# The start of a hybrid SSD and delta-rule step: x loaded in pieces from two queues, the first norm in halves, and the scaled x made on one engine

## The chip, the cores and the metric

The kernel runs on one core of one Trainium2 chip. The metric is device microseconds of one execution. The engines are PE (TensorE, matrix products and transposes), DVE (VectorE), ACT (ScalarE), POOL (GpSimd) and SP (SyncE, which here issues nearly all DMAs). DMAs can also be issued from ACT.

## What is computed

One inference step of a single-layer encoder. A prompt of 16 learned meta tokens and 256 tokens, and a sample of 64 tokens, 336 rows of 2048 in all, run through one layer:

```python
u = _rmsnorm(x, norm_mix_w)                     # x * rsqrt(mean(x*x) + EPS) * w, row by row
z_a, xbc_a, dt_a, qkv_b, z_b, beta_b, a_b, gate_a, gate_b = jnp.split(u @ w_in, SPLIT_IDX, axis=-1)
# branch A: causal conv, SiLU, SSD scan over blocks of 64, gated norm     -> ya
# branch B: causal conv, SiLU, gated delta rule over blocks of 64, norm   -> ob
mix = sigmoid(gate_a) * (ya @ w_out[:2048]) + sigmoid(gate_b) * (ob @ w_out[2048:])
h = x + mix
h = h + square(relu(_rmsnorm(h, norm_mlp_w) @ w_up)) @ w_down
```

Then a last RMSNorm. The outputs are y of the prompt and of the sample and the new conv and scan states of both. All data are float32.

## The kernel before

All 336 rows stand side by side on the free axis, and features on the partitions, 128 at a time. A float32 product is made of three: every operand is split into a rounded part (hi) and its rest (lo), and PE adds hi*hi, hi*lo and lo*hi. Weights come in a fixed stream of pieces of 512 KB (`stream`): `wload` (L193) loads piece n into one of three `raw` buffers, `wsplit` (L201) makes hi on ACT and lo on DVE (on POOL for n = 3) in three buffers each. `block` (L213) multiplies four pieces with all rows: at piece n it loads piece n + 3, whose buffer comes free when piece n is split, and splits the pieces up to n + 2. A piece feeds 24 matmuls.

This case is about the start, up to the first block of the first projection. Three tiles x0, x1, x2 of 112 rows each are loaded (`load_x`, L291; `segs` names the row ranges of the sources). For each tile the sum of squares is taken (`sumsq`, L321: x0 on ACT, x1 on DVE, x2 in halves on both), the root is made (`root`, L334: mean on DVE, power on POOL), 16 transposes on PE bring the tile to features on partitions (`flip`, L328, four at a time into one PSUM buffer) and ACT or DVE copies them to xT. A diagonal matrix of the roots (`spread_d`) is multiplied with ones on PE, so that the roots of all 336 rows stand on every partition: prx, copied to rbx. Then, for each of the 16 features groups k, `u_scale` (L380) makes ut = xT * rbx, and `u_split` (L384) makes uh on ACT and ul on DVE:

```python
def u_scale(k):
    ut[k] = sp0.tile([P, NT], F32, tag="ut", name="ut", bufs=6)
    tt(G if k % 2 else V, ut[k], xT[k // 4][:, k % 4, :], rbx, MUL)
```

The loop at L464 runs `u_split(k)` and `u_scale(k + 4)`, splits weight pieces 1 to 3 on the way, and issues two steps of three matmuls of block 0 for each k. Behind block 0, PE's order is written out: the transposes of small parameter rows to columns (pcol, from the loads cra, crb, sra, srb), the 32 matmuls of the token projection (ptok, with the weights wt split into wtr), and then the next blocks, pbig again.

From L344 to L472 the order on every engine is as written (`manual_schedule`). Instructions outside may be put among them: for all engines but PE a planner orders them ahead of the run by when it expects them to be ready, and by their place in the program among those that are ready. An engine then runs its instructions in that order, SP too. Before this stretch stand the loads of x and of prow; behind it, in the program's order: cra, crb, sra, srb, the two halves of dvec, four loads of pb, two of wt (L475 to L504). dvec, pb and wt are used by the scan, by `nega` (an Exp of pb on ACT, L528) and by the token projection. dvec is made of single floats, one half for each parity of the head:

```python
for h in range(2):
    nc.sync.dma_start(dvec[h * 64:(h + 1) * 64, :], i["ssd_d"][0].rearrange("(t h) -> h t", h=2)[h].partition_broadcast(64))
```

`scratch` (L996) stores the 16 tiles of xT to DRAM and clears twelve DRAM regions from the tile zero.

Of the kernel before, what the change touches and what calls it, by code (L numbers as in the profile page):

```python
# [8 lines left out]
F32 = mybir.dt.float32  # L9
F32R = mybir.dt.float32r  # L10
AF = mybir.ActivationFunctionType
ALU = mybir.AluOpType
# [3 lines left out]
D = 2048  # L16
KD = D // P
# [7 lines left out]
EPS = 1e-6  # L25
# [17 lines left out]
def tile_hybrid_step(ctx: ExitStack, tc: tile.TileContext, i: dict, o: dict):  # L43
    nc = tc.nc
# [9 lines left out]
    def scr(name):  # L54
        return pss.tile([P, 512], F32, tag="sc", name=name)

    def mm(out, lhsT, rhs, start=True, stop=True, **kw):
        nc.tensor.matmul(out, lhsT=lhsT, rhs=rhs, start=start, stop=stop, **kw)  # L58

    def act(out, in_, func=AF.Copy, **kw):  # L60
        nc.scalar.activation(out=out, in_=in_, func=func, **kw)  # L61

    def tt(eng, out, a, b, op):
        eng.tensor_tensor(out=out, in0=a, in1=b, op=op)  # L64
# [4 lines left out]
    V, G = nc.vector, nc.gpsimd  # L69
    MUL, ADD, SUB = ALU.mult, ALU.add, ALU.subtract  # L70
# [5 lines left out]
    ident = const.tile([P, P], F32, name="ident")  # L76
    make_identity(nc, ident)
    ones = const.tile([P, P], F32, name="ones")
# [6 lines left out]
    def transp(out, in_):  # L85
        n = in_.shape[0]
        nc.tensor.transpose(out, in_, ident[:n, :n])
# [10 lines left out]
    def new_u(name):  # L98
        return (keep.tile([P, KD, NT], F32R, tag="uh", name=name + "h"),
                keep.tile([P, KD, NT], F32R, tag="ul", name=name + "l"))  # L100

    uh, ul = new_u("u")
    acc = keep.tile([P, KD, NO], F32, name="acc")

    par = const.tile([P, 73], F32, name="par")
# [4 lines left out]
    dvec = const.tile([P, 16], F32, name="dvec")  # L110
# [82 lines left out]
    def wload(n):  # L193
        if n >= len(stream) or n in raws:
            return
        raw = wpool.tile([P, 4, 256], F32, tag="raw", name="raw", bufs=3)
        for c0, src in stream[n]:
            nc.sync.dma_start(raw[:, :, c0:c0 + src.shape[1]], src.rearrange("(k p) c -> p k c", p=P))
        raws[n] = raw

    def wsplit(n):  # L201
        if n >= len(stream) or n in split:
            return
        wload(n)
        hi = wpool.tile([P, 4, 256], F32R, tag="hi", name="hi", bufs=3)
        act(hi, raws[n])
        lo = wpool.tile([P, 4, 256], F32R, tag="lo", name="lo", bufs=3)
        tt(G if n == 3 else V, lo, raws[n], hi.bitcast(F32), SUB)
        split[n] = hi, lo
# [62 lines left out]
    sp0 = start.enter_context(tc.tile_pool(name="sp0", bufs=1))  # L272
# [3 lines left out]
    zero = sp0.tile([P, 4 * DG // P], F32, name="zero")  # L276
# [11 lines left out]
    xs = []  # L288
    segs = [[(0, "meta", 0, 16), (16, "pr", 0, 96)], [(0, "pr", 96, 112)], [(0, "pr", 208, 48), (48, "sa", 0, 64)]]
    src = {"meta": i["meta_tokens"], "pr": i["x_prompt"][0], "sa": i["x_sample"][0]}  # L290
    def load_x(n):  # L291
        for p0, s, r0, nr in segs[n]:
            nc.sync.dma_start(xs[n][p0:p0 + nr, :], src[s][r0:r0 + nr, :])

    for n in range(3):
        xs.append(xp.tile([112, D], F32, name=f"x{n}"))
    load_x(0)
    load_x(1)
    prow = sp0.tile([73, P], F32, name="prow")
    for r0, name, nr in ((NM, "norm_mix_w", 16), (SN, "ssd_norm_w", 16), (NP_, "norm_mlp_w", 16), (CB_, "ssd_conv_b", 24), (GN, "gdn_norm_w", 1)):  # L300
        nc.sync.dma_start(prow[r0:r0 + nr, :], i[name][0].rearrange("(t c) -> t c", c=P))
    load_x(2)
    warm = sp0.tile([P, 1], F32, name="warm")
    act(warm, ones[:, 0:1], AF.Square)

    def load_cols(dst, row, n):
        ps = scr("pcol")
        transp(ps[:, :n], row[:n, :])
        V.tensor_copy(dst, ps[:, :n])


    xT = [cpool.tile([P, 4, NT], F32, tag=t, name="xT", bufs=b) for t, b in (("q", 2), ("k", 2), ("v", 1))]
    xT.append(sp0.tile([P, 4, NT], F32, name="xT3"))
    junk = acc.rearrange("p k n -> p (k n)")[:112, :]
    ssx = sp0.tile([112, 4], F32, name="ssx")
    rsx = sp0.tile([112, 3], F32, name="rsx")
    dgx = sp0.tile([112, 3, 112], F32, name="dgx")
    rbx = sp0.tile([P, NT], F32, name="rbx")
    HD = D // 2

    def sumsq(f, x, d0, n):  # L321
        d = junk[:, d0:d0 + x.shape[1]]
        if f is act:
            act(d, x, AF.Square, accum_out=ssx[:, n:n + 1])
        else:
            V.scalar_tensor_tensor(out=d, in0=x, scalar=1.0, in1=x, op0=MUL, op1=MUL, accum_out=ssx[:, n:n + 1])

    def flip(n, k):  # L328
        ps = scr("pu").rearrange("p (k t) -> p k t", k=4)[:, :, :112]
        for m in range(4):  # L330
            transp(ps[:, m, :], xs[n][:, (k + m) * P:(k + m + 1) * P])
        return xT[k // 4][:, :, n * 112:(n + 1) * 112], ps

    def root(n):  # L334
        r = rsx[:, n:n + 1]
        V.tensor_scalar(out=r, in0=ssx[:, n:n + 1], scalar1=1.0 / D, scalar2=EPS, op0=MUL, op1=ADD)
        tt(G, r, r, nhalf_pow[:112, 0:1], ALU.pow)

    def spread_d(n):
        V.tensor_scalar(out=dgx[:, n, :], in0=ident[:112, :112], scalar1=rsx[:, n:n + 1], scalar2=None, op0=MUL)  # L340

    manual = ExitStack()
    manual.enter_context(tc.manual_schedule())

    pw_ = scr("pwarm")
    for n in range(8):
        mm(pw_[:, :P], ident, ident)
    prx = psb.tile([P, 512], F32, tag="big", name="prx")
    sumsq(act, xs[0], 0, 0)
    for k in range(0, KD, 4):  # L350
        (V.tensor_copy if k < 8 else act)(*flip(0, k))
    root(0)
    sumsq(V, xs[1], D, 1)
    for k in range(0, KD, 4):
        act(*flip(1, k))
    root(1)
    load_cols(par, prow, 73)
    for n in range(3):
        wload(n)
    sumsq(act, xs[2][:, :HD], 0, 2)  # L360
    sumsq(V, xs[2][:, HD:], D, 3)
    tt(V, ssx[:, 2:3], ssx[:, 2:3], ssx[:, 3:4], ADD)
    root(2)
    spread_d(0)
    spread_d(1)
    act(*flip(2, 0))
    late = [flip(2, k) for k in (4, 8, 12)]
    spread_d(2)
    wsplit(0)
    for n in range(3):  # L370
        mm(prx[:, n * 112:(n + 1) * 112], ones[:112, :], dgx[:, n, :])
    act(rbx, prx[:, :NT])
    for a in late:
        act(*a)
    xctx.close()
    sp = start.enter_context(tc.tile_pool(name="sp", bufs=1))
# [1 line left out]
    ut = {}  # L378

    def u_scale(k):  # L380
        ut[k] = sp0.tile([P, NT], F32, tag="ut", name="ut", bufs=6)
        tt(G if k % 2 else V, ut[k], xT[k // 4][:, k % 4, :], rbx, MUL)

    def u_split(k):  # L384
        t, w = ut.pop(k), par[:, NM + k:NM + k + 1]
# [76 lines left out]
    for k in range(4):  # L462
        u_scale(k)
    for k in range(KD):  # L464
        u_split(k)
        if k + 4 < KD:
            u_scale(k + 4)
        if k % 4 == 1 and k < KD - 4:
            wsplit(k // 4 + 1)
        for _ in range(2 if k < KD - 1 else 1):  # L470
            next(main0)
# [12 lines left out]
    srb_src = i["state_gdn_conv"][0, 0].rearrange("k (t c) -> (k t) c", c=P)  # L484
    for n in range(2):
        nc.sync.dma_start(srb[n], srb_src[n * 72:(n + 1) * 72, :])
    for h in range(2):
        nc.sync.dma_start(dvec[h * 64:(h + 1) * 64, :], i["ssd_d"][0].rearrange("(t h) -> h t", h=2)[h].partition_broadcast(64))
    pb = sp.tile([P, 2, 48], F32, name="pb")
# [16 lines left out]
    for n in range(2):  # L506
        w, wr = wt[:, n * 8:(n + 1) * 8, :], wpool.tile([P, 8, P], F32R, tag="hi", name="wtr", bufs=3)
# [697 lines left out]
    with tc.manual_schedule():  # L1205
        for t in range(3):
            final_part(7, t)
            r, n = frs[:, t:t + 1], toks[t][1]
            stt(r[n], fss[n, t, 7:8], 1.0 / D, fsum[n, t:t + 1], MUL, ADD)
            tt(G, r[n], r[n], nhalf_pow[n, 0:1], ALU.pow)  # L1210
        for m in range(2):
            for t, (_, n, t0) in enumerate(toks):
                dst = o["y_prompt"][0, t0:t0 + P, :] if t < 2 else o["y_sample"][0]
                w, r = slice(m * H, (m + 1) * H), frs[n, t:t + 1]
# [36 lines left out]
```

## Time and profile before

| | us |
|---|---|
| median of 3 runs (2331.62 to 2332.45) | 2331.97 |
| the profiled execution | 2331.78 |
| its span in the profile | 2330.1 |
| DVE busy | 1360.9 (58%) |
| ACT busy | 1064.6 (46%) |
| POOL busy | 333.0 (14%) |

The profile is of one execution. Times are counted from the start of the span; a busy PE is one that has matmuls in its pipeline, at whatever clock. PEclk is the granted clock of TensorE: 1.00 is 2.4 GHz, 0.50 is 1.2 GHz. A bracket behind a row tells how long the engine had been idle and what ended that.

### The profile page before, as it was taken

The page shows a single profiled execution, that of the slowest core. Times are in us where ns is not written, and L with a number is a line of the kernel's source. Part 1 is how long each engine was busy: PE and PEld are TensorE (multiplying, and loading weights), DVE is VectorE, ACT ScalarE, POOL GpSimd, SP SyncE. Part 2 cuts the span into 40 slices and gives each one's busy share as a digit, 9 for nine tenths or more (in the row PEclk, how much of TensorE's full clock was granted, in tenths as well). Part 3 has the DMA queues.
Part 4 walks back from the last instruction along what each step waited for, and adds up shares of the span by engine and source line. Part 5 has one row for each costly group of instructions (what it writes and reads, how often), then busy time and mean ns, then how long its engine had stood idle before and what let it go on. Part 6 is the DMA issues. An engine that isn't in the chain of part 4 may idle for free.

```text
span 2330.1 us, 40632 instructions
## 1 busy us (share of the span) xinstructions
PE 2300.5 (99%) x16393; PEld 2278.1 (98%) x16393; DVE 1360.9 (58%) x2147; ACT 1064.6 (46%) x1830; POOL 333.0 (14%) x488
## 2 busy tenths in 40 slices
PE   7999999999999999999999999999999999999997
PEld 7999999999999999999999999999999999999997
DVE  6674858585865547658668467444444444444444
ACT  5655546455445545554554445433343244324433
POOL 3151505041211102212212110000000000000000
PEclk8999999999999999999999999999999999999999
DMA  7846555545575555555546644544554444445543
GB/s 194 225 121 188 143 159 150 159 135 173 156 200 170 148 164 139 154 150 144 156 148 165 170 142 145 154 149 151 148 154 149 150 148 151 154 146 153 168 141 117
DMA packets 411046, 362.87 MB, mean 156 GB/s; under 512 B 48329, under 2 KB 407834, under 8 KB 410394
## 3 DMA queue, kind: packets, MB, share of 16 engines
q1 hardware_dynamic: 410746, 360.15, 53.1%
q8 instruction: 128, 2.10, 0.4%
q14 instruction: 60, 0.49, 0.1%
q10 hardware_dynamic: 112, 0.13, 0.0%
HBM read 340.57 MB, written 19.66 MB: 155 GB/s over the span
## 4 chain that ended last, share of the span: by engine, by line
PE 91%; DVE 5%; DMA 2%; issue 1%; SPq 1%; ACT 0%; ACTq 0%; POOL 0%; DVEq 0%
PE pbig L58 84%; DVE lo L64 1%; PE po L58 1%; DMA em<-rowd 1%; DVE pr L64 1%; DVE ubt L858 1%; PE pS L58 0%; PE pw L58 0%; PE pyd L58 0%; DVE c L67 0%; PE pkk L58 0%; PE pqk L58 0%; PE ph L58 0%; DMA x<-in_x_sample_dram 0%; PE pyo L58 0%
## 5 line engine op out<-in xcount | busy, mean ns | idle before, releaser
L64 DVE TENSOR_TENSOR lo<-raw,hi 128x1024 fp32r<-128x1024 f32 x591 | 739.1, 1251 | 697.3 <-ACT hi L61 688.0
L61 ACT ACTIVATE hi<-raw 128x1024 fp32r<-128x1024 f32 x592 | 626.3, 1058 | 892.1 <-PE pbig L58 834.6
L58 PE MATMUL pbig<-uh,hi 128*128 128x320 f32 (+2 forms) x2176 | 688.9, 317 | 3.1 <-ACT uh L61 3.1
L58 PE MATMUL pbig<-ul,hi 128*128 128x320 f32 (+2 forms) x2176 | 681.9, 313 | 2.9 <-DVE ul L67 2.7
L58 PE MATMUL pbig<-uh,lo 128*128 128x320 f32 (+2 forms) x2176 | 680.8, 313 | 1.6 <-DVE lo L64 1.6
L58 PEld LDWEIGHTS pbig<-uh,hi 128*128 128x128 f32 x2176 | 410.9, 189 | 9.1 <-ACT uh L61 3.8
L58 PEld LDWEIGHTS pbig<-ul,hi 128*128 128x128 f32 x2176 | 410.8, 189 | 4.7 <-DVE ul L67 4.3
L58 PEld LDWEIGHTS pbig<-uh,lo 128*128 128x128 f32 x2176 | 411.0, 189 | 2.4 <-DVE lo L64 2.4
L58 PE MATMUL pbig<-hh,hi 128*128 128x320 f32 x1024 | 318.0, 311 | 0.0
L58 PE MATMUL pbig<-hnl,hi 128*128 128x320 f32 x1024 | 317.1, 310 | 0.0
L58 PE MATMUL pbig<-hl,hi 128*128 128x320 f32 x1024 | 316.3, 309 | 0.0
L58 PE MATMUL pbig<-hh,lo 128*128 128x320 f32 x1024 | 316.2, 309 | 0.0
L58 PE MATMUL pbig<-hnh,lo 128*128 128x320 f32 x1024 | 315.8, 308 | 0.0
L58 PE MATMUL pbig<-hnh,hi 128*128 128x320 f32 x1024 | 315.1, 308 | 0.0
L58 PEld LDWEIGHTS pbig<-hnh,lo 128*128 128x128 f32 x1024 | 192.9, 188 | 0.0
L58 PEld LDWEIGHTS pbig<-hl,hi 128*128 128x128 f32 x1024 | 192.6, 188 | 0.0
L58 PEld LDWEIGHTS pbig<-hh,hi 128*128 128x128 f32 x1024 | 192.6, 188 | 0.0
L58 PEld LDWEIGHTS pbig<-hnh,hi 128*128 128x128 f32 x1024 | 192.4, 188 | 0.2
L58 PEld LDWEIGHTS pbig<-hh,lo 128*128 128x128 f32 x1024 | 192.5, 188 | 0.0
L58 PEld LDWEIGHTS pbig<-hnl,hi 128*128 128x128 f32 x1024 | 192.2, 188 | 0.0
L58 PE MATMUL pbig<-yh,hi 128*128 128x320 f32 x512 | 161.1, 315 | 0.0
L58 PE MATMUL pbig<-yh,lo 128*128 128x320 f32 x512 | 157.5, 308 | 0.0
(303 smaller groups left out, 2425.8 us busy)
## 6 DMA issues: line engine op xcount, KB each, us to landing
raw<-in_w_in_dram SPq DMA_DIRECT2D x256, 512.0 KB, 3.8
raw<-in_w_up_dram SPq DMA_DIRECT2D x128, 512.0 KB, 3.8
raw<-in_w_down_dram SPq DMA_DIRECT2D x128, 512.0 KB, 3.4
raw<-in_w_out_dram SPq DMA_DIRECT2D x64, 512.0 KB, 3.4
raw<-in_w_in_dram SPq DMA_DIRECT2D x32, 256.0 KB, 3.1
em<-rowd SPq DMA_DIRECT2D x8, 512.0 KB
u<-uD SPq DMA_DIRECT2D x4, 768.0 KB, 7.1
eab<-rowd SPq DMA_DIRECT2D x8, 336.0 KB, 6.9
```

The lines of the kernel that those rows point to most:

```text
L58: nc.tensor.matmul(out, lhsT=lhsT, rhs=rhs, start=start, stop=stop, **kw)
L61: nc.scalar.activation(out=out, in_=in_, func=func, **kw)
L64: eng.tensor_tensor(out=out, in0=a, in1=b, op=op)
L858: V.tensor_reduce(out=ubt[:NE, j0:, s], in_=v, axis=AX.X, op=ADD)
```

## The change

x is loaded in the order x0, x2, x1, each tile in four pieces of 512 columns (2 KB of a row): x0 and x2 from SP, x1 from ACT. All of it stands in an order written out. Each tile's sum of squares is taken in two halves, the first on ACT and the second on DVE, and `rooted` adds them before the mean and the power. The warm-up products on PE are 14 and not 8. The order of transposes, copies, squares and roots is new, the copies are shared out anew between DVE and ACT, the diagonal products are made tile by tile, and the weight loads 0 to 2 are issued ahead of the squares. All 16 products of xT and rbx are on DVE. Ahead of the loads of dvec, two small DVE operations write one column of dvec and of zero with zeros made from the last tile of uh.

```diff
-    load_x(0)
-    load_x(1)
+    start_order = ExitStack()
+    start_order.enter_context(tc.manual_schedule())
+    for n in (0, 2, 1):
+        for q in range(4):
+            w = slice(q * D // 4, (q + 1) * D // 4)
+            for p0, s, r0, nr in segs[n]:
+                (nc.scalar if n == 1 else nc.sync).dma_start(xs[n][p0:p0 + nr, w], src[s][r0:r0 + nr, w])
     prow = sp0.tile([73, P], F32, name="prow")
...
-    load_x(2)
+    start_order.close()
...
+    def sums(n, m):
+        sumsq((act, V)[m], xs[n][:, m * HD:(m + 1) * HD], m * HD, 2 * n + m)
+
+    def rooted(n):
+        tt(V, rsx[:, n:n + 1], ssx[:, 2 * n:2 * n + 1], ssx[:, 2 * n + 1:2 * n + 2], ADD)
+        r = rsx[:, n:n + 1]
+        V.tensor_scalar(out=r, in0=r, scalar1=1.0 / D, scalar2=EPS, op0=MUL, op1=ADD)
+        tt(G, r, r, nhalf_pow[:112, 0:1], ALU.pow)
+
+    def spread(n):
+        mm(prx[:, n * 112:(n + 1) * 112], ones[:112, :], dgx[:, n, :])
...
-    for n in range(8):
+    for n in range(14):
         mm(pw_[:, :P], ident, ident)
...
+    cp = V.tensor_copy
+    f0 = [flip(0, k) for k in (0, 4, 8, 12)]
+    sums(0, 0)
+    cp(*f0[0])
+    sums(0, 1)
+    rooted(0)
+    act(*f0[1])
+    f1 = [flip(1, k) for k in (0, 4)]
+    sums(1, 0)
+    sums(1, 1)
+    cp(*f0[2])
+    act(*f0[3])
+    f1 += [flip(1, k) for k in (8, 12)]
     spread_d(0)
+    spread(0)
+    rooted(1)
+    sums(2, 0)
+    cp(*f1[0])
+    f2 = [flip(2, 0)]
+    sums(2, 1)
+    rooted(2)
+    act(*f1[1])
+    f2.append(flip(2, 4))
     spread_d(1)
+    spread(1)
+    cp(*f1[2])
+    act(*f1[3])
+    f2 += [flip(2, k) for k in (8, 12)]
     spread_d(2)
+    spread(2)
+    load_cols(par, prow, 73)
+    act(*f2[0])
     wsplit(0)
...
     act(rbx, prx[:, :NT])
...
-        tt(G if k % 2 else V, ut[k], xT[k // 4][:, k % 4, :], rbx, MUL)
+        tt(V, ut[k], xT[k // 4][:, k % 4, :], rbx, MUL)
...
+    for t in (dvec, zero):
+        V.tensor_scalar(out=t[:, 0:1], in0=uh[:, KD - 1, 0:1].bitcast(F32), scalar1=0.0, scalar2=0.0, op0=ALU.min, op1=ALU.max)
     for h in range(2):
         nc.sync.dma_start(dvec[h * 64:(h + 1) * 64, :], i["ssd_d"][0].rearrange("(t h) -> h t", h=2)[h].partition_broadcast(64))
```

## Rows read from the trace of the kernel before

**Rows 1.** Page, part 1: busy us (share) xinstructions by engine.

```profile
PE 2300.5 (99%) x16393; PEld 2278.1 (98%) x16393; DVE 1360.9 (58%) x2147; ACT 1064.6 (46%) x1830; POOL 333.0 (14%) x488
```

**Rows 2.** Waits of PE from 53 us: total us, times, longest.

```profile
PE pbig L58 <- DVE lo L64: 1.6, 3, 0.7
```

**Rows 3.** Timeline of PE: start us, us, operation, xcount, [idle before].

```profile
1.58 3.78 PE L58 MATMUL pwarm<-ident 128*128 128x128 f32 x16 [1.58 <-POOL ident masks.py:199]
...
15.03 3.22 PE L87 MATMUL pu<-ident,x 112*128 112x112 f32 x16 [2.58 <-DMA x<-in_x_sample_dram]
...
21.84 0.65 PE L58 MATMUL pbig<-uh,hi 128*128 128x336 f32 x1 [2.30 <-ACT uh L61]
...
46.63 0.25 PE L87 MATMUL pcol<-ident,cra 96*128 96x96 f32 x1
...
48.39 0.40 PE L58 MATMUL ptok<-uh,wtr 128*128 128x336 f32 x1
...
53.41 0.32 PE L58 MATMUL pbig<-uh,hi 128*128 128x336 f32 x1
```

**Rows 4.** Waits of PE from 20 to 53 us.

```profile
PE pbig L58 <- ACT uh L61: 3.1, 2, 2.3
PE pbig L58 <- DVE ul L67: 2.7, 2, 2.1
PE pcol L87 <- DVE cwa L309: 1.1, 1, 1.1
```

**Rows 5.** Stretches: us, busy us by engine, PEclk, DMA share, GB/s.

```profile
6.00:10.00 4.00, 2.99 (x16) 2.90 (x16) 1.40 (x3) 2.48 (x3) 0.33 (x1) 1.00 1.11 278
...
15.00:18.00 3.00, 2.97 (x16) 3.00 (x17) 2.57 (x8) 2.54 (x4) 0.55 (x1) 0.50 1.09 349
...
22.00:28.00 6.00, 5.76 (x18) 4.90 (x19) 6.00 (x9) 4.85 (x9) 3.73 (x4) 0.50 0.44 120
...
38.00:45.00 7.00, 6.25 (x24) 5.71 (x24) 3.26 (x7) 2.11 (x5) 0.31 (x1) 0.54 1.12 199
...
30.00:36.00 6.00, 4.42 (x27) 3.86 (x26) 6.00 (x7) 2.27 (x4) 4.66 (x3) 1.00 0.05 0
```

**Rows 6.** Timeline of SP, its DMA issues.

```profile
6.89 0.65 SPq L293 DMA_DIRECT2D x<-in_x_sample_dram  x1
...
11.60 0.69 SPq L488 DMA_DIRECT2D dvec<-in_ssd_d_dram  x1
...
26.45 0.61 SPq L488 DMA_DIRECT2D dvec<-in_ssd_d_dram  x1
...
28.71 6.12 SPq L491 DMA_DIRECT2D pb<-in_gdn_dt_bias_dram  x1
...
43.35 8.30 SPq L999 DMA_DIRECT2D xTd<-xT  x16
...
53.88 5.48 SPq L198 DMA_DIRECT2D raw<-in_w_in_dram  x5
```

**Rows 7.** DMA packets from 28 to 36 us.

```profile
DMA packets 891, 0.04 MB, mean 5 GB/s; under 512 B 853, under 2 KB 890, under 8 KB 890
```

**Rows 8.** Timeline of ACT.

```profile
40.84 0.24 ACT L61 ACTIVATE nega<-pb 128x48 f32<-128x48 f32 x1 [7.39 <-DMA pb<-in_gdn_a_log_dram]
```

**Rows 9.** Timeline of DVE.

```profile
14.99 1.23 DVE L326 SCALAR_TENSOR_TENSOR acc<-x 112x1024 f32<-112x1024 f32 x1 [2.28 <-DMA x<-in_x_sample_dram]
...
26.60 0.50 DVE L64 TENSOR_TENSOR ut<-xT,rbx 128x336 f32<-128x336 f32 x1
27.02 1.04 DVE L67 SCALAR_TENSOR_TENSOR ul<-ut,par,uh 128x336 fp32r<-128x336 f32 x2
...
29.59 1.22 DVE L64 TENSOR_TENSOR lo<-raw,hi 128x1024 fp32r<-128x1024 f32 x1
...
34.39 3.13 DVE L67 SCALAR_TENSOR_TENSOR ul<-ut,par,uh 128x336 fp32r<-128x336 f32 x2
```

**Rows 10.** Waits of SP, 0 to 60 us.

```profile
SPq L293 <- DMA x<-in_x_prompt_dram: 2.0, 1, 2.0
```

More of the change, by code (lines that the diff above doesn't have):

```diff
@@ L290, in tile_hybrid_step @@
     src = {"meta": i["meta_tokens"], "pr": i["x_prompt"][0], "sa": i["x_sample"][0]}
-    def load_x(n):
-        for p0, s, r0, nr in segs[n]:
-            nc.sync.dma_start(xs[n][p0:p0 + nr, :], src[s][r0:r0 + nr, :])
     for n in range(3):
         xs.append(xp.tile([112, D], F32, name=f"x{n}"))
-    load_x(0)
-    load_x(1)
+    start_order = ExitStack()
[5 more added lines that the diff above has]
+                (nc.scalar if n == 1 else nc.sync).dma_start(xs[n][p0:p0 + nr, w], src[s][r0:r0 + nr, w])
     prow = sp0.tile([73, P], F32, name="prow")
@@ L314, in tile_hybrid_step @@
     junk = acc.rearrange("p k n -> p (k n)")[:112, :]
-    ssx = sp0.tile([112, 4], F32, name="ssx")
     rsx = sp0.tile([112, 3], F32, name="rsx")
@@ L332, in flip @@
         return xT[k // 4][:, :, n * 112:(n + 1) * 112], ps
[L334 to L337, printed above, removed]
     def spread_d(n):
         V.tensor_scalar(out=dgx[:, n, :], in0=ident[:112, :112], scalar1=rsx[:, n:n + 1], scalar2=None, op0=MUL)
+    ssx = sp0.tile([112, 6], F32, name="ssx6")
+    def sums(n, m):
[7 more added lines that the diff above has]
+        mm(prx[:, n * 112:(n + 1) * 112], ones[:112, :], dgx[:, n, :])
     manual = ExitStack()
@@ L345, in tile_hybrid_step @@
     pw_ = scr("pwarm")
-    for n in range(8):
+    for n in range(14):
         mm(pw_[:, :P], ident, ident)
     prx = psb.tile([P, 512], F32, tag="big", name="prx")
[L349 to L357, printed above, removed]
     for n in range(3):
         wload(n)
[L360 to L363, printed above, removed]
-    spread_d(0)
+    cp = V.tensor_copy
[11 more added lines that the diff above has]
+    f1 += [flip(1, k) for k in (8, 12)]
+    spread_d(0)
+    spread(0)
[7 more added lines that the diff above has]
+    f2.append(flip(2, 4))
     spread_d(1)
-    act(*flip(2, 0))
-    late = [flip(2, k) for k in (4, 8, 12)]
+    spread(1)
+    cp(*f1[2])
+    act(*f1[3])
+    f2 += [flip(2, k) for k in (8, 12)]
     spread_d(2)
+    spread(2)
+    load_cols(par, prow, 73)
+    act(*f2[0])
     wsplit(0)
-    for n in range(3):
-        mm(prx[:, n * 112:(n + 1) * 112], ones[:112, :], dgx[:, n, :])
     act(rbx, prx[:, :NT])
-    for a in late:
+    for a in f2[1:]:
         act(*a)
```

## The prediction

> **What bounds the kernel now.** I read the page's busy line first. PE is busy for 2300.5 of 2330.1 us [rows 1], so all that a change at the start can win is part of some 30 us, and only what moves PE's own work forward counts. The waits of PE tell where those 30 us are. After 53 us the largest group of waits is 1.6 us [rows 2]: from there the kernel is one stretch of matmuls, and what the start gains arrives whole at the end, unless a later wait takes it back. Before that PE has nothing of the projection to multiply until 21.84 us [rows 3]; then it waits 3.1 us for uh, 2.7 us for ul and 1.1 us for column copies [rows 4]. It also runs at half clock from 22 to 28 us and over most of 38 to 45 us [rows 5]: the second stretch holds 24 matmuls in 6.25 us, 0.26 us each, where the 32 matmuls of the token projection take 53.41 - 48.39 = 5.02 us, 0.157 each [rows 3].
>
> Two causes stand behind the stretch from 21.84 to 46.63, where block 0 ends and the column transposes begin [rows 3]. One is DVE, which makes the scaled x and ul and is busy without a gap from 22 to 28 and from 30 to 36 us [rows 5]. The other is SP's queue. After the second half of dvec (issued at 26.45) an issue hangs from 28.71 for 6.12 us, to 34.83 [rows 6], and from 30 to 36 us the queue moves 0 GB/s [rows 5]; 853 of the 891 packets between 28 and 36 us are under 512 B [rows 7], and only dvec, 1024 single floats in each half, has that many. Behind it come pb and wt. ACT has the Exp of pb in its order ahead of the last four uh and waits 7.39 us for it [rows 8], and the token projection, which needs wt, starts at 48.39 [rows 3]. The sum below is made against the profiled execution, 2331.78 us, 0.19 under the median of 2331.97.
>
> **Part 1, x in 2 KB pieces from two queues, squares in halves.** Now DVE starts on the last x at 14.99 us, when it lands [rows 9]; its last piece was issued only at 6.89 [rows 6], after SP waited 2.0 us for an earlier x to land [rows 10] (the tenth DMA waits for the second, so eight are in flight). After: 16 pieces on SP at 8.30 / 16 = 0.52 us [rows 6] are issued by 0.8 + 8.3 = 9.1 us, ACT's four beside them. 2.75 MB at the 278 GB/s that the queue has from 6 to 10 us [rows 5] take 9.9 us from 1.6 on, so 11.5; at the 349 GB/s from 15 to 18 us [rows 5], 9.5. If the limit of eight also holds up ACT's four issues, ACT's first square stands behind them, up to 2 us. I take 12.0, with 10.5 and 14 as ends.
>
> The 278 GB/s are one queue's. The Trainium skill (DMA: Bandwidth & Descriptors, "Issuing engines are not separate DMA queues") says that DMAs started by several engines run on the same 16 DMA engines and save only the time to issue. By that rule the second queue buys no rate and the sum stays as it is; by the rate of the weights 2 us more would be won, and it would end at 2324.5. The trace shows only one queue, so it does not decide.
>
> From the last x to the first matmul it is 21.84 - 14.99 = 6.85 us now. In that time the 16 transposes of the last x run to 18.25 [rows 3] and hold back the three matmuls that spread the roots; in pieces, they are done as the pieces land, and I take 1 us off: 5.85, so the first matmul is at about 18. Six more warm-up matmuls are 12 instructions at 3.78 / 16 = 0.24 us [rows 3], 2.8 us, of which PE's idle time up to the first x hides 1.6. If the clock stays at half level, all 48 transposes at 3.22 / 16 = 0.2 us [rows 3] take 9.7 us after 8.2, and the first matmul slips to 21. Ends: 16.5 and 21; taken 18, a gain of 3.8.
>
> **Part 2, all products on DVE.** A product alone takes DVE 0.50 us, and the next operation starts 0.42 after it; two ul behind it take 1.04, 0.52 each; a low half of the weights 1.22 [rows 9]. POOL's low half of the fourth weight piece stays, and beside it two ul take 3.13 us, 2.1 more [rows 9]. After the first ul come 16 x 0.52 + 12 x 0.42 (four products stand before it) + 2 x 1.22 + 2.1 = 17.8 us. From 18 on the last ul is done at 35.8, and block 0 ends one step later, at 36.8. PE's own sum: 6 us at half clock with 18 matmuls, as between 22 and 28 us [rows 5], then 78 x 0.157 = 12.2; 36.2, no tighter. It ends at 46.63 now. POOL's eight products no longer stretch the DVE operations beside them; if DVE stayed as slow as now with twice the products, the end would be near 39; with the first matmul at 16.5 it would be 35.
>
> **Part 3, dvec and zero written from the last uh.** The two small DVE operations cost under 0.5 us behind the last ul. They make both halves of dvec, and the loads that clear the scratch from zero, wait for uh's last tile. pb and wt, next in SP's order, then go ahead of dvec, and the 7.39 us on ACT [rows 8] go. What is late next is the column copies and the token projection: now 53.41 - 46.63 = 6.8 us [rows 3], 1.1 of it a wait for copies that stand behind wt's low half on DVE [rows 4]. I keep 6.2, so the token projection ends at 43.0, a gain of 10.4; with the ends of block 0, 8.2 to 12.2.
>
> What it costs: dvec is not gone. SP comes to it when DVE is through with ul, near 36, and both halves then follow each other. The one issued at 26.45 held the queue to 34.83, 8.4 us, or at the least for the 6.12 us of the hung issue [rows 6]. Two: 12.2 to 16.8 us, so that other loads move again at 48.2 to 52.8. Among them is the eighth weight piece, whose buffer comes free when the fifth is split; it was issued at 53.88 [rows 6], right behind the token projection, so near 43.5 after. PE wants it three pieces later, at 43.0 + 3 x 24 x 0.157 = 54.3. Moving from 52.8 on, 0.52 MB at 349 GB/s land at 54.3, 55.3 with one DMA ahead of it, and two splits of up to 1.22 us make it ready at 57.7: a wait of 3.4 us. By the lower end there is none. After waits of this size PE was at half clock from 38 to 45 us [rows 5], 24 x 0.10 = 2.4 us lost; I take 1.5 of it. So 4.9 us are given back (ends: 0, and 12 if SP has much else ahead of that piece).
>
> Sum: 10.4 - 4.9 = 5.5 us. 2331.78 - 5.5 = 2326.3; by the median, 2326.5.
>
> **Rivals.** *No giving back.* The weight pieces are issued ahead of dvec, or dvec's floats drain beside other traffic. For it: the first half, issued at 11.60 [rows 6] behind three weight pieces, held nothing up while these moved at 349 GB/s [rows 5]. Against it: the 0 GB/s from 30 to 36 us. Then 10.4 us stay: 2321.5.
>
> *The queue behind dvec.* The 16 stores of xT, 8.30 us of issues, and the loads that clear the scratch stand between dvec and the eighth weight piece. For it: now the stores go at 43.35, ahead of the weight pieces at 53.88 [rows 6]. Against it: they wait for nothing late, and without dvec SP has free time before 35 us. With half of them behind, 4.2 us more of waiting and 1 us more at half clock: 2331.5; with all, 2336.
>
> *Slower: wt behind dvec.* SP's order is fixed ahead of the run. If wt stands behind both halves, it leaves at 52.8, lands some 5 us later and is split by 60; the token projection starts there and not at 48.39, 11.6 us late, and with 2.4 us at half clock the time is 2346. It decides from the point where wt is issued behind the first half: the hold of 8.4 us is then in front of wt. Against it: the first half stands at 11.60, ahead of loads that the program names before it [rows 6], so the order goes by what is ready, and wt is ready 15 us before dvec.
>
> **How the numbers follow.** Forecast 0.42, at 2322 to 2330 by the ends of the first matmul and of dvec's hold. No giving back 0.18 (2319 to 2324). Queue behind dvec 0.24 (2327 to 2337). wt behind dvec 0.13. A start that brings nothing, 0.03. Some 0.2%, 4.7 us, is what a measurement of this kernel tells from no change. Faster by more: 0.36 of the forecast, 0.18 and 0.01, 0.55. Within: 0.06 + 0.18 + 0.03 = 0.27. Slower: 0.05 + 0.13 = 0.18. The range, 2320 to 2336, leaves out wt behind dvec and the outer ends.
>
> **What would show it.** First pbig matmul near 18 us; products of 0.50 us on DVE and none on POOL, last ul near 36; Exp of pb without a wait; wt issued before dvec; dvec issued near 36, then some 15 us in which SP's loads hang; one wait of PE of 2 to 4 us for a low half near 54 us and half clock behind it. Wrong would be a first matmul after 21 us, a token projection that starts later than 44 us, or no wait at all behind it.

## The result, and the profile after

The kernel after takes 2344.37 us (median of 4 runs, 2343.28 to 2345.42), the kernel before 2332.21 beside it: a ratio of 1.0052, 95% interval 1.0040 to 1.0064. It is 12 us slower, where 2326.5 was forecast and 2336 was the end of the range. The span of its profiled execution is 2342.1 us, 12.0 over that of before.

All of it is lost at the start: the last 2245 us take the same in both kernels. The first fence is the last 2245 us of the kernel before, the second the last 2245 us of the kernel after, which begin 12 us later (columns: stretch, length, busy us and instructions of PE, PEld, DVE, ACT and POOL, PEclk, DMA share, GB/s).

```profile
85.00:2330.00 2245.00, 2228.35 (x15980) 2209.15 (x15978) 1303.97 (x2041) 1014.88 (x1744) 308.51 (x437) 1.00 0.53 154
```

```profile
97.00:2342.00 2245.00, 2228.45 (x15982) 2209.47 (x15980) 1302.90 (x2041) 1014.80 (x1744) 309.19 (x439) 1.00 0.53 154
```

PE's busy time in them differs by 0.1 us. Ahead of them, this is the timeline of PE after, to be read beside [rows 3]:

```profile
22.39 0.65 PE L58 MATMUL pbig<-uh,hi 128*128 128x336 f32 x1 [2.49 <-ACT uh L61]
...
41.88 0.25 PE L87 MATMUL pcol<-ident,cra 96*128 96x96 f32 x1
42.70 0.40 PE L58 MATMUL ptok<-uh,wtr 128*128 128x336 f32 x1
...
47.72 0.32 PE L58 MATMUL pbig<-uh,hi 128*128 128x336 f32 x1
...
73.19 0.65 PE L58 MATMUL pbig<-uh,hi 128*128 128x336 f32 x1 [13.34 <-ACT hi L61]
74.44 0.65 PE L58 MATMUL pbig<-uh,lo 128*128 128x336 f32 x1 [0.33 <-DVE lo L64]
...
84.94 0.56 PE L58 MATMUL pcum<-la,tri 80*80 80x48 f32 x4 [1.72 <-DVE la L64]
```

and this the row of before that answers to its last one (no wait stands between 53.41 and it):

```profile
72.66 0.50 PE L58 MATMUL pcum<-la,tri 80*80 80x48 f32 x4
```

The first large matmul is 0.5 us later than before. Block 0 ends 4.75 us earlier, but for its last three matmuls, which stand behind the token projection and with which the row at 47.72 begins; PE comes to that row 5.69 us earlier. At the cumulative sum of the gates (pcum) PE is 12.28 us late, so 17.97 us are lost between 47.72 and 84.94. The three waits hold 13.34 + 0.33 + 1.72 = 15.39 of them. Half clock holds most of the rest:

```profile
42.00:58.00 16.00, 15.86 (x107) 15.60 (x106) 8.58 (x21) 7.41 (x13) 1.25 (x8) 1.00 0.05 1
73.20:77.70 4.50, 4.17 (x14) 3.74 (x15) 4.23 (x9) 4.09 (x8) 0.00 (x0) 0.50 0.95 270
```

Behind the wait, 14 matmuls take 4.5 us at PEclk 0.50; at 0.157 each [rows 3] they would take 2.2, so 2.3 are lost, the wait of 0.33 among them. The first line is why PE waits: through 16 us the DMA engines move 1 GB/s at a busy share of 0.05. Timeline of SP after, its DMA issues:

```profile
11.92 0.52 SPq L299 DMA_DIRECT2D x<-in_x_sample_dram  x1
...
14.78 1.50 SPq L198 DMA_DIRECT2D raw<-in_w_in_dram  x3
...
40.14 1.42 SPq L513 DMA_DIRECT2D dvec<-in_ssd_d_dram  x2
41.60 13.01 SPq L1024 DMA_DIRECT2D xTd<-xT  x7
61.32 1.61 SPq L1029 DMA_DIRECT2D aD<-zero  x3
62.97 1.82 SPq L1029 DMA_DIRECT2D uD<-zero  x3
64.92 5.55 SPq L198 DMA_DIRECT2D raw<-in_w_in_dram  x5
```

Waits of SP after from 36 us, DMA packets from 44 to 58 us, and the row of ACT that waits for the eighth weight piece:

```profile
SPq L1029 <- DMA dvec<-in_ssd_d_dram: 6.6, 1, 6.6
```

```profile
DMA packets 1503, 0.01 MB, mean 0 GB/s; under 512 B 1503, under 2 KB 1503, under 8 KB 1503
```

```profile
72.08 1.06 ACT L61 ACTIVATE hi<-raw 128x1024 fp32r<-128x1024 f32 x1 [20.73 <-DMA raw<-in_w_in_dram]
```

Read together: both halves of dvec leave at 40.14, as soon as the two guard writes are done. In 14 us 1503 packets of 4 bytes move, 9.3 ns each, and nothing else does. A share of 0.05 is less than that of one of 16 engines that is always busy (0.0625), so they move as if one after the other: 2048 x 9.3 ns = 19.1 us, from 41 to 60. Seven stores hang behind them, a clearing load waits until they have landed, six clearing loads of 258 KB go first, and the eighth weight piece is issued at 64.92, 11 us later than before [rows 6], and is usable at 73.19.

The rate was in the trace of before as well: 853 small packets in 8 us [rows 7] are 9.4 ns each. There the halves stood 15 us apart [rows 6], and the first half held other loads up too. It moved once the weight pieces ahead of it were through, and from 19 to 21 us of before nothing else moved:

```profile
DMA packets 195, 0.00 MB, mean 0 GB/s; under 512 B 195, under 2 KB 195, under 8 KB 195
```

### The profile page after: what moved, and what is told of

Read it like the earlier page. It is cut to its first block, busy times and chain, and to the rows that moved or that the text cites. A ratio compares the mean times of both kernels' runs of the same rounds, so it can differ in the third digit from the quotient of the medians.

```text
span 2342.1 us, 40697 instructions
## 1 busy us (share of the span) xinstructions
PE 2298.4 (98%) x16405; PEld 2275.7 (97%) x16405; DVE 1358.9 (58%) x2163; ACT 1064.5 (45%) x1830; POOL 323.5 (14%) x480
## 4 chain that ended last, share of the span: by engine, by line
PE 91%; DVE 4%; DMA 3%; issue 1%; SPq 0%; ACT 0%; POOL 0%; ACTq 0%; DVEq 0%
PE pbig L58 84%; DVE lo L64 1%; DMA xTd<-xT 1%; PE po L58 1%; DMA em<-rowd 1%; DVE ubt L883 1%; DMA raw<-in_w_in_dram 1%; DVE pr L64 1%; PE pS L58 0%; PE pw L58 0%; DVE c L67 0%; PE pyd L58 0%; PE pkk L58 0%; PE pqk L58 0%; PE ph L58 0%
## 5 line engine op out<-in xcount | busy, mean ns | idle before, releaser
L58 PE MATMUL pbig<-uh,hi 128*128 128x320 f32 (+2 forms) x2176 | 688.2, 316 | 15.8 <-ACT hi L61 13.3
```

## The experiments

Medians of 4 to 12 runs each, with the ratio to the kernel before, measured in turns on the same chip (its median 2332.05 to 2332.48), and its 95% interval; *first*, *block 1* and *pcum* are PE's milestones as above, in one profiled execution each. In the six kernels whose first stage is that of before, *first* lies between 20.60 and 22.21, so a difference of 1 us between two single executions says little.

| kernel | us | ratio | first | block 1 | pcum |
|---|---|---|---|---|---|
| before | 2332.2 | | 21.84 | 53.41 | 72.66 |
| after | 2344.37 | 1.0052 (1.0040 to 1.0064) | 22.39 | 47.72 | 84.94 |
| after_dvec_rows | 2331.80 | 0.9997 (0.9988 to 1.0006) | 22.99 | 48.33 | 71.60 |
| after_rows_late_copy | 2326.22 | 0.9976 (0.9967 to 0.9985) | 22.74 | 48.08 | 67.92 |
| before_dvec_rows | 2327.22 | 0.9978 (0.9968 to 0.9987) | 21.63 | 48.81 | 68.04 |
| after_dvec_act_queue | 2344.25 | 1.0049 (1.0036 to 1.0061) | 22.61 | 47.96 | 85.00 |
| after_dvec_half | 2337.04 | 1.0018 (1.0009 to 1.0027) | 23.01 | 48.35 | 79.40 |
| after_no_guard | 2339.57 | 1.0029 (1.0017 to 1.0040) | 22.98 | 61.87 | 81.80 |
| after_rows_no_guard | 2326.48 | 0.9977 (0.9967 to 0.9987) | 22.83 | 49.45 | 68.75 |
| before_rows_products_guard | 2332.10 | 1.0000 (0.9991 to 1.0009) | 21.68 | 47.85 | 71.00 |
| before_rows_products_guard_late | 2324.93 | 0.9969 (0.9958 to 0.9981) | 20.60 | 45.41 | 65.35 |
| before_rows_dve_products | 2324.96 | 0.9967 (0.9956 to 0.9979) | 22.11 | 46.91 | 66.22 |
| after_rows_pool_products | 2329.59 | 0.9990 (0.9982 to 0.9999) | 23.91 | 52.18 | 71.85 |
| before_rows_products_lo_dve | 2323.79 | 0.9970 (0.9952 to 0.9989) | 22.21 | 45.95 | 66.00 |
| after_rows_whole_loads | 2331.14 | 0.9997 (0.9988 to 1.0006) | 22.73 | 49.56 | 70.83 |
| after_rows_whole_no_guard | 2325.81 | 0.9972 (0.9962 to 0.9982) | 22.66 | 49.27 | 68.56 |
| after_rows_early_columns | 2328.70 | 0.9984 (0.9975 to 0.9992) | 24.64 | 49.45 | 68.75 |

**The floats of dvec.** after_dvec_rows loads the vector as 128 rows of 128 bytes and takes dvec out of them by two copies:

```diff
-    for h in range(2):
-        nc.sync.dma_start(dvec[h * 64:(h + 1) * 64, :], i["ssd_d"][0].rearrange("(t h) -> h t", h=2)[h].partition_broadcast(64))
+    nc.sync.dma_start(drow, i["ssd_d"][0].partition_broadcast(P))
...
+    for h in range(2):
+        V.tensor_copy(dvec[h * 64:(h + 1) * 64, :], drow[h * 64:(h + 1) * 64, :].rearrange("p (t h) -> p h t", h=2)[:, h, :])
```

> The changed kernel, but ssd_d is loaded as 128 rows of 32 floats in one DMA to a tile drow and split to dvec by two DVE copies; the two small DVE writes go to drow and zero, so the load stands in SP's order where dvec stood (7 stores of xT before it, 7 and the clearing loads behind it). Theory A (dvec's 2048 single floats hold SP's loads for 20 us, 41 to 61, and the eighth weight piece stands behind them): PE's wait of 13.3 us for hi and the half clock behind it go; 2344.4 - 13.3 - 2.3 - 1.7 = about 2327. Rival B (the stores of xT and the clearing loads ahead of that piece are the hold, by their bytes): the wait stays at 8 us or more, 2337 to 2344.

The wait of 13.3 us is gone and 12.6 us with it, but not down to 2327: another wait stands ahead of pcum, and half clock behind it (timeline of PE and of ACT in that kernel):

```profile
71.60 0.93 PE L58 MATMUL pcum<-la,tri 80*80 80x48 f32 x4 [3.87 <-DVE la L64]
```

```profile
58.98 1.06 ACT L61 ACTIVATE hi<-raw 128x1024 fp32r<-128x1024 f32 x1 [2.14 <-DMA raw<-in_w_in_dram]
59.94 0.31 ACT L61 ACTIVATE e<-e 128x144 f32<-128x144 f32 x1
```

The same load in the kernel before, before_dvec_rows:

> The kernel before with the same row load of ssd_d, nothing else. Theory A: the hold from 28.7 to 34.8 us goes, pb and wt land early, ACT's Exp no longer waits 7.4 us; DVE then sets the end of block 0 near 42 us instead of 46.6, and the token projection follows at once: 5 to 6 us less, about 2326.5. Rival B: the order of loads, not dvec, makes pb and wt late: within 1 us of before, 2332.

2327.2: five of the 2332.2 us of before are made by the single floats of dvec, whose second half stands in front of pb and wt. nega then runs at 33.12 without a wait, where it waited 7.39 us [rows 8].

Is it SP's queue that hangs, or the engines? after_dvec_act_queue issues the floats from ACT (nc.scalar for nc.sync in the load of dvec):

> The changed kernel with both halves of dvec, still as single floats, issued from ACT's queue, behind the last wtr on ACT. If the hold is in SP's queue (what stands behind dvec on SP cannot start), the weights pass: 2326 to 2328 as with rows. If the single floats fill a DMA engine that every load needs, the weights still wait, with the full 20 us or a part of it: 2333 to 2344.

The time does not change. SP's stores, which no longer stand behind dvec in one queue, take 18.8 us to issue 14, and PE waits for the same piece (timeline of SP, waits of PE from 42 us, waits of SP from 36 us):

```profile
34.44 18.82 SPq L1024 DMA_DIRECT2D xTd<-xT  x14
53.36 8.97 SPq L1029 DMA_DIRECT2D aD<-zero  x3
```

```profile
PE pbig L58 <- ACT hi L61: 13.2, 1, 13.2
```

```profile
SPq L1029 <- DMA dvec<-in_ssd_d_dram: 7.7, 1, 7.7
SPq L1024 <- DMA dvec<-in_ssd_d_dram: 4.3, 1, 4.3
```

So a place of their own in another queue does not help, and SP still waits for dvec to land before it issues more, 4.3 and 7.7 us. That the floats fill one DMA engine, the second theory, does not follow, and the trace of before speaks against it. From 18.8 us to the landing of the first half at 26.4 (11.60 + 14.8) 735 small packets move, so at least 289 of its 1024 floats had moved already. They did so behind the weight pieces, where from 18.2 to 18.8 us 364 small packets went, 1.6 ns each (first fence; second, 18.8 to 26.4). At 9.4 ns one engine would have moved 64.

```profile
DMA packets 497, 0.14 MB, mean 229 GB/s; under 512 B 364, under 2 KB 497, under 8 KB 497
```

```profile
DMA packets 1312, 0.47 MB, mean 62 GB/s; under 512 B 735, under 2 KB 1312, under 8 KB 1312
```

Nor would one full engine keep the others from the seven stores of the kernel after: from 42.2 to 59.3 us all 1833 packets are under 512 B, and a store's have 1280. A step ahead of the engines that hands the floats out one by one would fit both; no run shows it. The hold is not always complete either: in this run other packets move at 41 GB/s from 49 to 53 us, and in the kernel before at 74 GB/s from 21 to 26, beside the floats. So at which step the floats hold the others up stays open; that they do, the kernels with rows show. after_dvec_half loads half of dvec as floats and the other half from rows:

> The kernel after, with one half of dvec (64x16) still loaded as single floats and the other half taken from a load of 128 rows of 32 floats by a copy on DVE. Theory A (each half of single floats fills one DMA engine for about 10 us, and the eighth weight piece waits for what is behind it): the stretch without bytes after dvec is about 10 us instead of 20, the matmuls' wait for the eighth piece falls from 13.3 us to 2 to 5, and the time is 2333 to 2338 us. Rival B (the single floats cost a fixed time, whatever their number): the wait stays at 12 to 14 us and the time at 2343 to 2345. Rival C (beyond a small number nothing is left to wait for): no wait, and the time is that with no single floats, 2331.8.

The stretch in which no bytes move is 8.1 us (42.7 to 50.8) where it was 17.1 (42.2 to 59.3), so the hold goes by the number of floats, as A says. The rest of A is not borne out, though the time is in its range: PE's wait of 8.2 us, from 48.98 to 57.15, is not for the eighth weight piece but for the fifth, and for the eighth it does not wait at all. This wait is a fault of the kernel: the copy out of drow stands on DVE behind a load that the floats hold up (9.7 us), and ACT, which makes the fifth piece's hi only at 56.05, waits for what is behind the copy.

**The guard.** after_no_guard takes the two small writes away from the kernel after, floats and all:

> The changed kernel without the two small DVE writes of dvec and zero. The order then has both halves of dvec right behind the first three weight loads. Theory A: a hold of 16 to 20 us from about 19 us on, the fourth weight piece, the column rows, pb and wt land after 36 us, block 0 ends near 47 and the token projection starts near 50: no wait at the eighth piece, 2333 to 2338. Rival (the guard only adds a wait, the early loads drain unseen): under 2330.

Both halves now leave at 17.10, and the floats hold up the loads of the first stage: 1524 small packets from 22 to 36 us, PE's wait for uh behind the fourth weight piece is 12.5 us, and block 1 starts at 61.87. The floats cost their hold at this place too; the time is 4.8 us under the kernel after, and 1.6 over A's range (block 0 ends at 56.02, where A said near 47). The same two lines left out with rows, after_rows_no_guard:

> The kernel after with dvec from rows and without the guard: loading in pieces, halves of the norm and products on DVE stay. Theory A (the guard is what the 6.9 us between the kernel after with rows, 2331.8, and the kernel before with rows and the products on DVE, 2325.0, is mostly made of: it holds the clearing loads and the vector's load back to about 40 us, and puts them in front of the weight pieces): 2326 to 2328.5 us, the wait of 3.87 us before the gates' cumulative sum goes, and that sum starts near 68. Rival B (the order of the first stage, with the parameters' column copy and the first lo behind the third norm, makes up the difference): 2330 to 2332, block 0 still ends at 42.5.

and the guard added to a kernel that lacks it, before_rows_products_guard:

> The kernel before with dvec from rows and all products on DVE (2325.0 us), and the guard of the change alone added to it (one element of the vector's tile and one of the zero tile written from the last uh). Theory A (the guard costs what the difference above is made of): 2328 to 2331 us, with a wait before the gates' cumulative sum of over 2 us. Rival B (without single floats the guard is free): 2324.5 to 2326 and no wait there.

In the two pairs the guard seems to cost 5.3 and 7.1 us, with a wait of 3.7 to 3.9 us ahead of pcum. That would make it a second cause. But the kernels with rows have two copies that the kernel after lacks, placed ahead of the token projection and, with the guard, behind a late load. In them, but for after_rows_pool_products below, ACT has the Exp e behind a weight piece's hi (59.94 above); in the kernel after and in the kernels without guard it stands in front of it. after_rows_late_copy moves the copies to the end of the start:

```diff
+    for h in range(2):
+        V.tensor_copy(dvec[h * 64:(h + 1) * 64, :], drow[h * 64:(h + 1) * 64, :].rearrange("p (t h) -> p h t", h=2)[:, h, :])
     start.close()
```

> The kernel after with dvec from a load of 128 rows of 32 floats, and the two copies that take dvec out of it moved to the end of the start, so that ACT's order and SP's are those of the kernel after and only the form of the one load differs. Theory A (in the first kernel with rows the copies, placed ahead of the token projection and behind a late load, turned the order on ACT and DVE round, put an Exp behind a weight piece's hi and made the 3.87 us wait; the guard itself costs nothing once the floats are gone): no wait over 1 us before the gates' cumulative sum, that sum at 67 to 68.5, and the time is 2325.5 to 2328 us, 16 to 19 less than the kernel after. Rival B (the guard's own order costs the 5 us): 2330.5 to 2332.5, with the wait.

> The kernel before with dvec from rows, all products on DVE and the guard (2332.1 us), with the two copies moved to the end of the start. Theory A (the copies' place made the 7.1 us that the guard seemed to cost): 2324 to 2326 us and no wait over 1 us before the gates' cumulative sum. Rival B (the guard): 2331 to 2333 with that wait.

2326.2 and 2324.9: A in both. These are all waits of PE in after_rows_late_copy from 20 to 90 us, and the Exp e with the hi next to it (timeline of ACT):

```profile
PE pbig L58 <- ACT uh L61: 2.5, 1, 2.5
PE pbig L58 <- DVE ul L67: 2.5, 3, 1.8
PE pbig L58 <- DVE lo L64: 0.3, 1, 0.3
```

```profile
57.62 0.32 ACT L61 ACTIVATE e<-e 128x144 f32<-128x144 f32 x1
57.84 1.04 ACT L61 ACTIVATE hi<-raw 128x1024 fp32r<-128x1024 f32 x1
```

With the copies at the end the guard costs nothing that these runs can tell: 2324.93 with it and 2324.96 without, 2326.22 with it and 2326.48 without, where the kernels without it have the copies at their early place. The form of dvec's load makes 2344.4 - 2326.2 = 18.1 us, and the 5.3 and 7.1 us that two pairs of runs had put on the guard were made by the copies that the experiment itself brought in. It is not their time on DVE: they run at 44.53 in after_dvec_rows and at 44.38 and 45.05 in after_rows_late_copy. What their place in the program changes is the order that the planner makes around them.

**The products on DVE.** before_rows_dve_products is before_dvec_rows with tt(V, ...) for tt(G if k % 2 else V, ...), and nothing else of the change:

> The kernel before with dvec from rows (2327.2 us) and the second part of the change alone: all products of x and root on DVE. Theory A (that part is worth its 1.85 us of the stage, and no more): block 0 ends at 41.0 to 41.4 instead of 42.97, block 1 starts 1.5 to 2 us earlier, and the time is 2325.2 to 2326.2 us. Rival B (what block 1 gains, the weight pieces behind it give back): block 1 starts earlier but the gates' cumulative sum does not, and the time is 2327 to 2328.

Block 1 starts 1.9 us earlier, pcum 1.8, and the time is 2.3 us less, 0.2 more than A said: A, though the intervals of the two ratios overlap. The reverse, after_rows_pool_products:

> The kernel after with dvec from rows (2331.8 us) and the products of x and root again in turns on POOL and DVE; the loading in pieces, the halves of the norm and the guard stay. Theory A (the products on DVE are the one part that shortens block 0): block 0 ends at 43.9 to 44.6 instead of 42.5, and the time is 2332 to 2334 us. Rival B (DVE's longer queue is what makes the gates late, 3.87 us of wait before the cumulative sum): that wait falls under 2 us and the time is 2329 to 2331.

Block 0 ends at 45.18, 2.7 us later, as A says, yet the time is 2.2 us less, as B says: the order with the long wait, which the copies had made, is not there in this kernel. So it tells of the products only beside after_rows_late_copy, which lacks that wait too: from the first matmul to the end of block 0 it is 21.3 us with POOL's products and 19.5 without. before_rows_products_lo_dve also moves POOL's one lo of a weight piece to DVE (V for G if n == 3 else V in wsplit):

> The kernel before with dvec from rows and all products on DVE (2325.0 us), and the one lo that POOL still makes (2.6 us there, and DVE's ul beside it stretches from 0.56 to 2.67 us) made on DVE in 1.22 us. Theory A (POOL's lo and DVE's operation share something, and the matmuls' wait of 1.48 us before the ul is all due to that): the wait falls under 0.5 us, block 0 ends at 39.9 to 40.4 instead of 41.07, and the time is 2323.8 to 2324.6. Rival B (DVE is the bound of the stage, and 1.22 us more on it costs as much as the stretch): block 0 ends at 40.9 to 41.4 and the time is the same within 0.4 us.

Block 0 ends at 40.1, 1 us earlier, PE's waits for ul are 1.0 in place of 1.5 us, and the time is 1.2 us less, within the interval. This is the lowest median of all, 2323.79 us, but its ratio of 0.9970 (0.9952 to 0.9989) can't be told from those next to it.

**The first stage.** after_rows_whole_loads loads x as before, in whole rows from SP:

> The kernel after with dvec from rows (2331.8 us) and x loaded again as before: whole rows of 8 KB, all from SP. The halves of the first norm on ACT and DVE, the products on DVE and the guard stay. Theory A (the pieces cost the front its gain: x0's last piece is issued at 6.9 us and the first weight piece at 15.3): the first weight piece is issued near 10 us, the first large matmul is at 20.5 to 21.3 instead of 23.0, block 0 ends at 40 to 41.2 instead of 42.5, and the time is 2329 to 2331 us. Rival B (halves of the norm on two engines are what is late): the first large matmul stays at 22.5 to 23.2 and the time at 2331 to 2332.

The first weight piece is issued at 10.23 and not at 15.28, and still the first large matmul is at 22.73: B. This kernel has the guard and the copies, and the wait ahead of pcum with them (1.9 us). Without the guard, after_rows_whole_no_guard:

> The kernel after with dvec from rows, without the guard (2326.5 us), and with x loaded in whole rows from SP as before; the halves and the order of the first norm and the products on DVE stay. Theory A (the last x lands by the rate of the 16 engines, 223 to 228 GB/s in both forms, so the pieces win nothing, and the new order of the norm costs 1.2 us by the column copy and the first lo behind the third norm): first large matmul at 22.5 to 22.9, and the time is 2326 to 2327 us. Rival B (the pieces cost what the front loses): first large matmul under 22.2 and 2324.5 to 2325.5.

A by the first matmul, 22.66; the time, 2325.8, lies 0.2 under A's range, and the intervals don't tell it from the 2326.5 of the pieces. What holds the first matmul (timeline of DVE):

```profile
17.49 0.28 DVE L334 TENSOR_SCALAR dgx<-ident,rsx 112x112 f32<-112x112 f32 x1
20.21 0.23 DVE L309 COPY par<-pcol 128x73 f32<-128x73 f32 x1 [2.44 <-PE pcol L87]
20.36 1.22 DVE L64 TENSOR_TENSOR lo<-raw,hi 128x1024 fp32r<-128x1024 f32 x1
21.50 1.76 DVE L64 TENSOR_TENSOR ut<-xT,rbx 128x336 f32<-128x336 f32 x4
```

The copy of the parameter columns stands behind the third norm and waits for PE; the first lo and the products come behind it. In before_rows_dve_products that lo runs at 17.84, the products at 20.32. after_rows_early_columns moves the copy forward, without the guard and with whole loads:

```diff
     rooted(1)
+    load_cols(par, prow, 73)
     sums(2, 0)
...
     spread(2)
-    load_cols(par, prow, 73)
```

> The kernel after with dvec from rows, x in whole rows from SP as before, no guard, and the parameters' column copy moved from behind the third norm to behind the first root; the halves of the norm and the products on DVE stay. Theory A (behind the third norm the copy held up DVE's first lo and the products by 1.2 us; the halves of the first two norms are off the path, since the third norm ends the stage and had halves already): the first large matmul is at 21.3 to 22.2 instead of 22.73, block 0 ends at 40.5 to 41.4, and the time is 2324 to 2325.5 us, that of the kernel before with rows and products on DVE. Rival B (the halves themselves cost or gain): a first large matmul over 22.4 with 2326 or more, or under 21 with less than 2324.

A is wrong: the first matmul is at 24.64 and the time 2328.7. These are the numbers of B, but not by B's cause. PE's transpose of the columns now waits 3.69 us for a copy on ACT that stands behind ACT's square of the last x, and DVE waits 4.70 us for the transpose, ahead of its own half of that square:

```profile
17.06 0.23 DVE L309 COPY par<-pcol 128x73 f32<-128x73 f32 x1 [4.70 <-PE pcol L87]
17.21 0.61 DVE L378 COPY xT<-pu 128x448 f32<-128x448 f32 x1
17.74 1.22 DVE L325 SCALAR_TENSOR_TENSOR acc<-x 112x1024 f32<-112x1024 f32 x1
```

Whether the copy at some other place makes the new norm faster than the old one was not tried.

## Why the prediction was wrong

- **Part 1, first matmul at 18: wrong.** It came at 22.39, past the 21 us that the prediction names as a sign of being wrong. The last x was to land at 12.0, by the 278 GB/s of one stretch of 4 us. Its last packet moves at 14.0 us in both kernels, and from 1.6 to 14 us before (first fence) and after (second) move nearly the same:

```profile
DMA packets 587, 2.83 MB, mean 228 GB/s; under 512 B 138, under 2 KB 251, under 8 KB 251
```

```profile
DMA packets 1688, 2.76 MB, mean 223 GB/s; under 512 B 331, under 2 KB 344, under 8 KB 1688
```

Pieces and a second queue win no rate. The Trainium skill says so of queues (DMA: Bandwidth & Descriptors, "Issuing engines are not separate DMA queues"); the trace agrees. The way from the last x to the first matmul was to fall from 6.85 to 5.85 us, as its transposes would be done while the pieces land. DVE starts its last square at 15.18 without waiting for a load, and from there it is 7.21: eight transposes still run from 17.65, ahead of the last spread, and the column copy and the first lo stand in front of the products (timeline of PE after, then of DVE):

```profile
17.65 1.70 PE L87 MATMUL pu<-ident,x 112*128 112x112 f32 x8
19.15 0.63 PE L58 MATMUL prx<-dgx,ones 112*128 112x112 f32 x2
```

```profile
15.18 1.22 DVE L326 SCALAR_TENSOR_TENSOR acc<-x 112x1024 f32<-112x1024 f32 x1
...
19.94 0.23 DVE L310 COPY par<-pcol 128x73 f32<-128x73 f32 x1 [2.15 <-PE pcol L87]
20.09 1.21 DVE L64 TENSOR_TENSOR lo<-raw,hi 128x1024 fp32r<-128x1024 f32 x1
```

SP issues its last piece at 11.92, held 4.0 us by x landing, and the weights only behind it, at 14.78. The gain of 3.8 was none.
- **Part 2, 17.8 us from the first to the last ul: right.** (Its terms add up to 17.9.) From 22.39 to 40.06 is 17.7, with products of 0.50 and the stretch beside POOL's lo of 2.7 us. Against the same kernel with POOL's products it is worth 2.3 us.
- **Part 3, pb and wt ahead of dvec: right.** nega runs at 31.01 without a wait, wt is issued at 27. The next block starts 5.7 us early where 10.4 was forecast; the first matmul's 4.4 us make up nearly all of the difference.
- **The eighth weight piece ready at 57.7: the step that failed.** It was usable at 73.19. Of the 15.5 us, 4.1 are dvec leaving at 40.14 and not near 36. The hold was taken as 12.2 to 16.8 us, from one issue that hung; by the packets of [rows 7], 9.4 ns x 2048, it is 19.2, and SP could go on only 21.2 us after the issue, 4.4 over the upper end. The other 7.0 are the queue, for which the forecast had one DMA: seven stores and six clearing loads stand in front of that piece. The rival *queue behind dvec* had this mechanism at 0.24, but its price of 4.2 to 8.3 us was the issuing time of the stores. What counts is that the clearing loads wait for dvec to land, until 61.32, then 3.6 us of issues, and then 1.5 MB that move ahead of the weight piece, 7.2 us from its issue to hi.
- **Half clock behind that wait, 1.5 us: about right,** 2.0.
- **The rival no giving back** rests on a wrong reading: the first half of dvec did hold loads up, from 19 to 21 us, and landed 14.8 us after its issue. While the weights moved at 349 GB/s, its floats hardly moved.
- **The rival wt behind dvec** did not happen; the slower side was reached by another queue.

With the floats gone the change takes 2326.2 (after_rows_late_copy), 6.3 us under before. That the forecast was 2326.5 is luck: it was 10.4 us won and 4.9 given back, with the floats in place. 5.0 of the 6.3 come from the vector's form alone, as before_dvec_rows shows, and 2.3 from the products. The guard adds nothing. The new first stage takes back some 1.3, less than the intervals can tell; the first matmul is at 22.39 to 23.01 in the seven kernels with all of it, later than in any of the six with the old one.

## What to carry to other kernels

Price a load by the packets that it makes: a vector of single floats, 8 KB in all, kept all other loads and stores from moving for 17 us, and the trace showed the nanoseconds of one packet before the change was made. When a load is moved back in a queue that runs in order, list what is issued behind it, up to the transfer that the busiest engine needs next, and price that transfer by landing, not by issue. When an experiment replaces an operation, compare the order on every engine with the kernel it stands for: two copies of 0.17 us each moved an Exp behind a weight piece and looked like a cost of 5 to 7 us of something else.

## What the runs showed of the hardware

- 4-byte pieces with a stride between them go at 9.2 to 9.4 ns each in four stretches (1503 in 14 us, 1524 in 14 us, 853 in 8 us, 637 in 6 us) at a DMA share of 0.05, below one engine of 16, and the hold is as long when ACT issues them. The Trainium skill (DMA: Bandwidth & Descriptors, "Rules for kernel authors") says that a strided last dimension is one descriptor per element; the counts agree (1833 of the 2048 in 17.1 us). That they run on one engine is not shown: in the kernel before 364 small packets went in 0.6 us.
- In the kernel after, stores issued behind them move only when they are nearly through: 0 to 1 GB/s for 17 us at a share of 0.05. In two other stretches loads or stores did move beside floats, at 41 and 74 GB/s.
- A DVE operation beside POOL's lo of 2.6 us stretches from 0.56 to 2.68 us. With that lo on DVE, which takes 1.22 us more there, the stretch is gone and block 0 ends 1 us earlier.
